# A two-layer hybrid decoder on one core: a new ordering model, turned forms by TensorE and ScalarE, and GpSimd's products on VectorE

## The chip, the cores and the metric

The kernel runs on one core of a Trainium2 chip. The metric is the device time of one execution in microseconds, from the first instruction to the last with what lies around them; lower is better. A run is one execution, and the number quoted for a kernel is the median of its runs. The engines have short names in the rows: PE is TensorE (PEld its weight loads), DVE is VectorE, ACT is ScalarE, POOL is GpSimd, SP is the queue that issues the DMAs.

## The reference

Two layers work on a residual stream of 512 tokens by 1024 channels. Each layer projects the stream once and gives the result to four token mixers on their own heads: A is a gated delta rule in chunks of 64 tokens, B is attention with low-rank queries and keys, C is a gated linear recurrence (HGRN2), D is dilated attention over three windows. Their outputs are joined, projected back and normalised, and a feed-forward block of width 4096 follows.

```python
for l in range(DEPTH):
    h = x @ w_in[l]
    ...
    o_a = _gated_deltanet(a_qkv, a_a, a_b, a_z, gdn_conv_w[l], gdn_a_log[l], gdn_dt_bias[l], gdn_norm_g[l])
    o_b = _mla(b_cq, b_ckv, b_kr, mla_q_norm_g[l], mla_kv_norm_g[l], mla_w_uq[l], mla_w_ukv[l], pos)
    o_c = _hgrn2(c_q, c_f, c_i, c_g, lower_bounds[l], hgrn_norm_g[l])
    o_d = _dilated_attention(d_qkv)
    mixed = jnp.concatenate([o_a, o_b.astype(x.dtype), o_c, o_d], axis=-1) @ w_out[l]
    x = _layer_norm(DEEPNORM_ALPHA * x + mixed, ln1_g[l], ln1_b[l])
    x = _layer_norm(DEEPNORM_ALPHA * x + _sq_relu_mlp(x, w_ff1[l], w_ff2[l]), ln2_g[l], ln2_b[l])
```

Inside A each chunk inverts a unit lower triangular matrix of 64 by 64, and the state runs from chunk to chunk.

## The kernel before

Activations lie with channels on the 128 partitions and the 512 tokens along the row. Every large product is made of three (high by high, high by low, low by high) from a split of both factors into a rounded part `H` and a rest `L`; `wh` and `wl` are the two parts of a weight tile, `xH` and `xL` those of the stream, and `mm`, `a`, `b`, `o` are the names of the eight PSUM buffers by use. A weight tile costs a DMA (`wr`), a rounding on ScalarE (`wh`) and a subtraction on VectorE (`wl`).

The program is first recorded as a list of operations with their dependences. A planner then goes through a model of the engines in time and picks, step by step, the operation that can start first. Its ties and its preferences come from a priority: the place in the list plus a `BIAS` by mixer and engine. `FILL`, `EMA`, `BURST`, `PATIENCE` and `DENSE` tell it when to prefer products of the full array, and `HOP`, `LEAVE`, `ENTER`, `WINDOW`, `DOWN`, `UP` are the figures of its model. The order found is then emitted engine by engine and fixed; on the chip each engine runs its own list from the front, and semaphores do the rest. So a number in the planner moves instructions all over the program, and no instruction overtakes another of its engine at run time.

The steps that the prediction speaks of, by their tile names:

- `sqh`, `sql`: the two parts of the squares for the norms of B; TensorE sums them over partitions (`a<-sqh,oner`, `a<-sql,oner`).
- `ktok`, `vtok` (mixer A) and `vt`, `kt` (mixer C): token-major forms, for each chunk of 64 tokens a 64 by 64 matrix turned on both halves of the partitions. `to_tokens` makes each with eight VectorE transposes of 32-row blocks. `ke` and `kd` are `ktok` times decays.
- `dt`, `db`, `LT`, `N`, `X`, `W`, `TB`, `T`, `U`: the decay matrices of A and the inverse of its triangular matrix. VectorE inverts blocks of 16 in 15 steps, writes `T` and `U` by block transposes, and TensorE then joins the blocks by small products (`a<-T,N`, `a<-Y,U`, `a<-U,Y`, `a<-T,LT`). The prediction calls this the `T` step.
- `qh`: the queries of B, products of PSUM tiles with a table on VectorE.
- `qa`, `kr`, `tot`, `sc`: queries, keys, running decay and scores of C, in six levels (`b<-qa,kr` are its score products).
- `at`, `as`, `tt`: scores, sums and turned weights of both attentions; `dk`, `dq`, `dl`, `dv` and `dtab` belong to D.
- `gm`: the gated output of A and C, split into `mixH` and `mixL` for the output projection.
- `o<-wh,mixH` and the like: the last of the three groups of the output projection, which the layer norm (`xt`, `lns`, `lny`) of the same 128 tokens follows.

GpSimd does elementwise products: `gm`, `qd`, `dt`, `db`, `t`, `N`, `kd`, `st`, `fl`, `kr`, `tot`.

```python
key = (t, e == "pe" and (dense or 0 < run < BURST) and ops[i][9] < DENSE, ops[i][8])
if pick is None or key < pick[0]:
    pick = (key, i, new)
```

Of the kernel before, what the change touches and what calls it, by code (L numbers as in the profile page):

```python
# [10 lines left out]
FR = mybir.dt.float32r  # L11
# [148 lines left out]
class Plan:  # L160
# [4 lines left out]
    TO_PE = 70.0  # L165
    LEAVE, ENTER = 95.0, {(128, 128): 105.0}
    WINDOW, DOWN, UP = 3413.0, 0.29, 0.65

    def __init__(self, nc):
        self.nc, self.ops, self.tiles = nc, [], 0  # L170
        self.kinds, self.queues, self.stream, self.bias = {}, {}, "", 0
        self.quota, self.reserve, self.fifo = {}, {}, set()
        self.ties, self.tied = {}, None
# [33 lines left out]
    def cost(self, e, method, out, ins, k):  # L207
        n = math.prod(out.shape[1:])
        psum = any(v.buf.kind == "ps" for v in [out, *ins])
        if e == "pe":  # L210
            if method == "transpose":
                return 109.0
            w, x = k["lhsT"], k["rhs"]
            n, m = math.prod(x.shape[1:]), w.shape[1]
            if w.dt == FR:
                return max(n * 0.4167 + 13.5, 109.0)
            t = 2 * max(2 * n * 0.4167 + 3, 2 * min(m, n) * 0.4167 + 3, 25.0)
            if w.shape[0] <= 64 or m <= 64:
                return t - 12 if out.span()[0] < 64 else 12.0
            return t  # L220
        if e == "ve":
            if method == "transpose":
                wide = len(out.shape) > 2 and out.shape[1] == 8
                return 446.0 if wide else 1045.0
            if method in ("tensor_scalar", "tensor_copy") and not psum:
                return 64 + 0.52 * n
            if method == "memset":
                return 30.0
            if method == "reciprocal":
                return 68 + 6.3 * n  # L230
            if method == "scalar_tensor_tensor" and not psum and n > 64:
                return 95 + 1.1 * n
            if method == "tensor_tensor_reduce":
                return 195 + 1.045 * n
            return 67 + 1.045 * n
        if e == "ac":
            if method == "dma_start":
                return 60.0
            ap = sum(not isinstance(k.get(w, 0.0), (int, float)) for w in ("bias", "scale"))
            acc = 90.0 if k.get("accum_out") is not None else 0.0  # L240
            return (51 if psum else 93) + (60 * ap if n <= 128 and psum else 93 * ap) + acc + 0.833 * n
        if e == "po":
            if method == "tensor_scalar":
                return 150 + 4.2 * n
            return 190 + 2.2 * n
        return 450.0

    def tile_of(self, method, k):
        if method == "transpose":
            return (128, 128)  # L250
        if method != "matmul":
            return None
        grid = lambda c: 32 if c <= 32 else 64 if c <= 64 else 128
        return grid(k["lhsT"].shape[0]), grid(k["lhsT"].shape[1])

# [7 lines left out]
    def record(self, e, method, a, k):  # L263
# [8 lines left out]
        ins = [v for v in [*a[1:], *k.values()] if isinstance(v, View) and not any(v is o for o in outs)]  # L272
# [32 lines left out]
        if self.tied is not None and e.name == "pe":  # L305
            self.tied.append(i)
        self.ops.append([e, method, a, k, deps, list(bufs.values()), cost, tail, i + self.bias + BIAS.get((self.stream, e.name), 0),
                         self.activity(e, method, k, cost), self.tile_of(method, k)])

    def order(self):  # L310
# [18 lines left out]
        warm, dense, mode, run, forced = False, True, None, 0, None  # L329
# [44 lines left out]
        while done < n:  # L374
            best = None
            for e, cand in avail.items():
                pick = None
                for i in cand if forced is None or e != "pe" else (forced,):
                    t = max(at[e], ready[i])
                    new = [b for b in ops[i][5] if not b.held]  # L380
# [20 lines left out]
            t = max(at[e], ready[i])  # L401
            for kd in {b.kind for b in new}:
                t = max(t, sorted(slots[kd])[sum(b.kind == kd for b in new) - 1])
# [9 lines left out]
            if e == "pe":  # L413
# [5 lines left out]
                if not warm:  # L419
                    cost, work = 2 * cost, 2 * work  # L420
                if mode is not None and op[10] != mode:
                    t = max(t, at[e] + self.LEAVE)
                    cost += self.ENTER.get(op[10], 50.0)
                mode, forced = op[10], self.ties.get(i)
                run = run + 1 if op[9] >= DENSE else 0
                busy += work
                gap = math.exp(-(t - at[e]) / EMA)
# [3 lines left out]
            at[e] = t + cost  # L431
            self.warm[i] = warm
            end[i] = at[e]
# [9 lines left out]
            for j in users[i]:  # L443
# [6 lines left out]
                ready[j] = max(ready[j], end[i] + lat)  # L450
# [24 lines left out]
def emit(ctx, tc, io, layers=DEPTH):  # L475
# [133 lines left out]
    for l in range(layers):  # L609
# [6 lines left out]
        def gated(ot, gate, gain, k, tag):  # L616
# [7 lines left out]
            po.tensor_tensor(m, ot, sq, OP.mult)  # L624
# [108 lines left out]
        kq = [big("kq", [128, 8, 2, 64]) for _ in range(2)]  # L733
        vtok, z = [None, None], [None, None]
        bx = row("bx")
        def a_proj(name, o=None):
# [31 lines left out]
            dst = kq[p][:, :, 1 if name[1] == "q" else 0, :]  # L768
# [83 lines left out]
        for p in range(2):  # L852
# [10 lines left out]
            po.tensor_tensor(v3(qd[p]), kq[p][:, :, 1, :], v3(eg), OP.mult)  # L863
# [4 lines left out]
            po.tensor_tensor(v3(dt), v3(dt), rep(incl), OP.mult)  # L868
            db = row("db")
            po.tensor_tensor(v3(db), v3(dt), spread(beta[:, :, p]), OP.mult)  # L870
            QK[p] = row("QK")
            for nh in range(2):
                o = ps("a", (128, 4, 2, 64))
                for i in range(4):
                    for h in range(2):
                        b = kq[p][half[h], 4 * nh + i]
                        pe.matmul(o[half[h], i], lhsT=b[:, 0, :], rhs=b, start=True, stop=True)
# [49 lines left out]
        po.tensor_tensor(t1[r], bx[r], qtab[r], OP.mult)  # L927
        po.tensor_tensor(t2[r], bx[r], ktab[r], OP.mult)
# [47 lines left out]
        for p in range(2):  # L976
# [3 lines left out]
            po.tensor_tensor(Nv, pn(LT, p), rep(lev), OP.mult)  # L980
# [21 lines left out]
            to_tokens(v3(ktok), kq[p][:, :, 0, :])  # L1002
            ve.tensor_tensor(v3(ke), v3(ktok), spread(ce[:, 0, :, p]), OP.mult)
            po.tensor_tensor(v3(kd[p]), v3(ktok), spread(ce[:, 1, :, p]), OP.mult)
# [8 lines left out]
        for n in range(8):  # L1013
# [28 lines left out]
            else:  # L1042
                po.tensor_tensor(new, st, spread(ce[:, 2, n]), OP.mult)
# [22 lines left out]
        for name in W_TILES[9:17]:  # L1066
# [4 lines left out]
            if name[1] == "f":  # L1071
# [4 lines left out]
                po.tensor_tensor(fl, fl, e, OP.add)  # L1076
# [8 lines left out]
            elif name[1] == "i":  # L1085
# [3 lines left out]
                to_tokens(v3(vt[p]), v3(t))  # L1089
# [7 lines left out]
        for p in range(2):  # L1097
# [10 lines left out]
            for i in range(6):  # L1108
# [18 lines left out]
                po.tensor_tensor(kv[:, :, 0], kv[:, :, 0], spread(tv[:, :, 1], b), OP.mult)  # L1127
                nt_ = plan.tile("row" if nb > 64 else "sm", [128, nb], FT, "tot")
                po.tensor_tensor(nt_, tv[:, :, 0], tv[:, :, 1], OP.mult)
                tot = nt_  # L1130
            kt = row("kt")
            to_tokens(v3(kt), v3(kr[p]))
# [296 lines left out]
```

## Time and profile before

| | |
|---|---|
| median of three runs | 1382.39 us (1381.54 to 1384.11) |
| the profiled execution | 1383.82 us, span of its instructions 1382.0 us |
| mean granted clock of TensorE | 0.985 |
| busy: TensorE, VectorE, ScalarE, GpSimd | 1336.3, 784.7, 596.6, 91.4 us |

The span runs from the first to the last instruction of the profiled execution; the difference to its own time is what lies around it. An engine is busy while an instruction of its own runs; waiting for a semaphore is idle time, and the trace names the engine whose work ended it. Products on TensorE overlap, so the length of one says less than the distance from one start to the next. Layer 0 runs to about 675 us, and its feed-forward block begins at about 350 us.

### The profile page before, as it was taken

Reading aid. Unit: us, or ns where it says so; the run is one execution under the profiler, and the core shown is the slowest. Engines: PE = TensorE matmul, PEld = TensorE weight load, DVE = VectorE, ACT = ScalarE, POOL = GpSimd, SP = SyncE. Lnnn points to the kernel's source line nnn. Section 1 sums busy time; section 2 is a strip of 40 time slices with the busy share of each in tenths; the row PEclk is TensorE's granted clock in tenths of the full one; section 3 lists DMA queues with packets and bytes.
Section 4 is the critical chain, followed back from the end, with each engine's and each line's share of the span. In section 5 each row is a group of like instructions: output and inputs, shape, how many; then the busy total and the mean of one; then the engine's idle time right before and its main releaser. Section 6 shows DMA issues by size and latency. Waiting matters only on the chain.

```text
span 1382.0 us, 21797 instructions
## 1 busy us (share of the span) xinstructions
PE 1336.3 (97%) x8860; PEld 1084.0 (78%) x8860; DVE 784.7 (57%) x1533; ACT 596.6 (43%) x1124; POOL 91.4 (7%) x108
## 2 busy tenths in 40 slices
PE   8899999999999999999998989999999999999997
PEld 7657778778888888888886678787788888888886
DVE  6989585567743334422479898846658333344226
ACT  6643456548432223321485434656374322233112
POOL 0222020010000000000003212200000000000000
PEclk9999999999999999999999999999999999999999
DMA  6122201232542223324122242021415323232341
GB/s 225 40 88 77 82 4 47 77 122 74 165 141 93 92 92 94 105 92 155 59 92 62 92 146 71 3 69 69 135 64 189 116 92 92 92 106 92 126 149 61
DMA packets 44164, 132.65 MB, mean 96 GB/s; under 512 B 4896, under 2 KB 5152, under 8 KB 44064
## 3 DMA queue, kind: packets, MB, share of 16 engines
q1 hardware_dynamic: 44064, 131.27, 29.5%
q8 instruction: 69, 1.13, 0.3%
q14 instruction: 31, 0.25, 0.1%
HBM read 122.86 MB, written 8.39 MB: 95 GB/s over the span
## 4 chain that ended last, share of the span: by engine, by line
PE 76%; DVE 14%; ACT 7%; issue 2%; DMA 1%; POOL 0%; SPq 0%; DVEq 0%; POOLq 0%; ACTq 0%
PE mm L472 42%; PE a L472 17%; PE b L472 16%; ACT lny L472 2%; DVE wl L472 1%; DVE xt L472 1%; DVE y L472 1%; ACT wh L472 1%; DVE vtok L472 1%; PE o L472 1%; DVE ktok L472 1%; ACT scr L472 1%; ACT sg L472 1%; ACT xH L472 1%; DVE X L472 1%
## 5 line engine op out<-in xcount | busy, mean ns | idle before, releaser
L472 DVE TENSOR_TENSOR wl<-wr,wh 128x1024 fp32r<-128x1024 f32 (+1 forms) x195 | 237.6, 1222 | 360.4 <-ACT wh L472 355.1
L472 ACT ACTIVATE wh<-wr 128x1024 fp32r<-128x1024 f32 (+1 forms) x195 | 204.7, 1054 | 528.6 <-PE mm L472 501.1
L472 PE MATMUL mm<-xH,wl 128*128 128x512 f32 (+1 forms) x832 | 328.0, 395 | 0.0
L472 PE MATMUL mm<-xL,wh 128*128 128x512 f32 (+1 forms) x832 | 326.6, 393 | 0.0
L472 PE MATMUL mm<-xH,wh 128*128 128x512 f32 (+1 forms) x832 | 325.7, 392 | 0.7 <-DVE as L472 0.4
L472 PEld LDWEIGHTS mm<-xH,wh 128*128 128x128 f32 x832 | 157.9, 190 | 38.1 <-issue 1.9
L472 PEld LDWEIGHTS mm<-xL,wh 128*128 128x128 f32 x832 | 157.5, 190 | 38.1 <-issue 2.3
L472 PEld LDWEIGHTS mm<-xH,wl 128*128 128x128 f32 x832 | 157.6, 190 | 34.8 <-issue 1.6
L472 DVE TENSOR_TENSOR hL<-h,hH 128x512 fp32r<-128x512 f32 x64 | 41.8, 687 | 73.4 <-PE mm L472 73.2
L472 PE MATMUL b<-wh,hL 128*128 128x512 f32 x192 | 74.8, 390 | 0.0
L472 PE MATMUL b<-wh,hH 128*128 128x512 f32 x192 | 74.8, 390 | 0.0
L472 PE MATMUL a<-wh,hH 128*128 128x512 f32 x192 | 74.8, 389 | 0.0
L472 PE MATMUL a<-wl,hH 128*128 128x512 f32 x192 | 74.8, 389 | 0.0
L472 PE MATMUL b<-wl,hH 128*128 128x512 f32 x192 | 74.7, 389 | 0.0
L472 PE MATMUL a<-wh,hL 128*128 128x512 f32 x192 | 74.7, 389 | 0.0
L472 PE MATMUL mm<-wh,hH 128*128 128x512 f32 x128 | 49.9, 390 | 0.0
L472 PE MATMUL mm<-wh,hL 128*128 128x512 f32 x128 | 49.8, 389 | 0.0
L472 PE MATMUL mm<-wl,hH 128*128 128x512 f32 x128 | 49.8, 389 | 0.0
L472 ACT ACTIVATE at<-at,as 128x512 f32<-128x512 f32 (+3 forms) x64 | 35.7, 558 | 27.6 <-DVE as L472 27.5
L472 ACT ACTIVATE hH<-h 128x512 fp32r<-128x512 f32 x64 | 37.3, 619 | 15.4 <-DVE h L472 15.2
L472 DVE TENSOR_TENSOR h<-h,mm 128x512 f32<-128x512 f32 x60 | 40.6, 680 | 3.6 <-ACT h L472 3.6
L472 PEld LDWEIGHTS a<-wl,hH 128*128 128x128 f32 x192 | 36.1, 188 | 7.6
(292 smaller groups left out, 2275.8 us busy)
## 6 DMA issues: line engine op xcount, KB each, us to landing
wr<-in_w_ff_dram SPq DMA_DIRECT2D x128, 512.0 KB, 3.6
wr<-in_w_in_dram SPq DMA_DIRECT2D x47, 512.0 KB, 3.6
wr<-in_w_out_dram SPq DMA_DIRECT2D x16, 512.0 KB, 3.6
x<-xt SPq DMA_DIRECT2D x24, 256.0 KB, 2.1
xt<-x SPq DMA_DIRECT2D x24, 256.0 KB, 5.8
ln<-in_ln_dram SPq DMA_DIRECT2D x16, 256.0 KB, 5.5
x<-in_xT_dram SPq DMA_DIRECT2D x8, 256.0 KB, 6.1
dtab<-in_tabs_dram SPq DMA_DIRECT2D x8, 256.0 KB, 4.0
```

Source lines behind the costliest of these rows:

```text
L472: getattr(e.real, method)(*[real(v) for v in a], **{n: real(v) for n, v in k.items()})
```

## The change

There are three parts. First, the planner's model and its numbers: a matrix product now holds only the 32 by 32 cells of the array that it uses, so that products on other cells may follow at once; VectorE and GpSimd wait for each other in the model where an operation `shares` their port; activity of TensorE is counted by `streaming`; and `FILL`, `BURST`, `DOWN`, `UP` and `BIAS` have new values. Second, `turn` takes the place of `to_tokens` in four places: four TensorE transposes of 128 by 128 into one PSUM tile, and four ScalarE copies of 64 rows by 256 columns out of it; `kq` is laid out with keys and queries apart. Third, all products of GpSimd are VectorE's; GpSimd keeps only the fills of `TB`, `T` and `U`.

```diff
-FILL = (0.3, 0.5)
+FILL = (0.2, 0.30000000000000004)
 EMA = 2000.0
-BURST = 2
+BURST = 1
...
-BIAS = {('A0', 'ac'): -50, ('B', 've'): 600, ('C0', 've'): 200, ('D', 'ac'): -200}
+BIAS = {('', 've'): -750, ('A', 'po'): -800, ('A', 've'): 50, ('A0', 'ac'): 500, ('A0', 've'): 300,
...
-    WINDOW, DOWN, UP = 3413.0, 0.29, 0.65
+    WINDOW, DOWN, UP = 3413.0, 0.36, 0.38
...
+    def shares(self, e, method, ins, out):
+
+        inside = [v for v in ins if v.buf.kind != "ps"]
+        if e == "po":
+            return bool(inside)
+        if e != "ve":
+            return False
+        return len(inside) > 1 or (method in ("tensor_scalar", "tensor_copy") and len(inside) == 1 and out.buf.kind != "ps")
...
+    def streaming(self, e, method, k):
+
+        if e.name != "pe":
+            return 0.0
+        if method == "transpose":
+            return 107.0
+        w, n = k["lhsT"], math.prod(k["rhs"].shape[1:])
+        return n * 0.4167 * (1 if w.dt == FR else 4) * w.shape[0] / 128
...
+                    if e == "pe":
+                        t = max(t, drained) if turn else max(t, max(free[c] for c in ops[i][12]))
...
+    def turn(dst, src, tag):
+
+        o = ps(tag, (128, NT, 128))
+        for m in range(NT):
+            pe.transpose(o[:, m], src[:, 128 * m:128 * m + 128], ident)
+        d = dst.rearrange("q (m c) i -> q m c i", c=2)
+        for h in range(2):
+            for c in range(2):
+                ac.activation(d[half[h], :, c], o[half[c], :, 64 * h:64 * h + 64], AF.Copy)
...
-            po.tensor_tensor(m, ot, sq, OP.mult)
+            ve.tensor_tensor(m, ot, sq, OP.mult)
...
-        kq = [big("kq", [128, 8, 2, 64]) for _ in range(2)]
+        kq = [big("kq", [128, 2, 8, 64]) for _ in range(2)]
...
-                to_tokens(v3(vtok[p]), v3(y))
+                turn(v3(vtok[p]), y, "a")
...
-            po.tensor_tensor(v3(qd[p]), kq[p][:, :, 1, :], v3(eg), OP.mult)
+            ve.tensor_tensor(v3(qd[p]), kq[p][:, 1], v3(eg), OP.mult)
...
-            po.tensor_tensor(v3(dt), v3(dt), rep(incl), OP.mult)
+            ve.tensor_tensor(v3(dt), v3(dt), rep(incl), OP.mult)
...
-            po.tensor_tensor(Nv, pn(LT, p), rep(lev), OP.mult)
+            ve.tensor_tensor(Nv, pn(LT, p), rep(lev), OP.mult)
...
-            to_tokens(v3(ktok), kq[p][:, :, 0, :])
+            turn(v3(ktok), kq[p][:, 0].rearrange("q n i -> q (n i)"), "a")
...
-                po.tensor_tensor(kv[:, :, 0], kv[:, :, 0], spread(tv[:, :, 1], b), OP.mult)
+                ve.tensor_tensor(kv[:, :, 0], kv[:, :, 0], spread(tv[:, :, 1], b), OP.mult)
...
-            to_tokens(v3(kt), v3(kr[p]))
+            turn(v3(kt), kr[p], "b")
```

Three places of the order show what moves. In each row stand the operation, what it writes from what, and the shape of what it writes (a count at the end for equal rows in a run).

The first place is VectorE in mixer A and B's norms of layer 0, some 75 rows into its list. Before:

```order
L472 TENSOR_TENSOR dt<-a,ct_635 128x512
L472 TENSOR_SCALAR dt<-dt 128x512
L472 TENSOR_TENSOR ke<-ktok,ce 128x512
L472 STREAM_TRANSPOSE ktok<-kq 32x8x32 x4
L472 TENSOR_TENSOR sql<-bsq,sqh 128x512
L472 TENSOR_TENSOR ke<-ktok,ce 128x512
L472 TENSOR_TENSOR wl<-wr,wh 128x1024
L472 TENSOR_TENSOR sql<-bsq,sqh 128x512
```

And now, at the second `sql` of that shape:

```order
L522 TENSOR_TENSOR wl<-wr,wh 128x1024
L522 TENSOR_TENSOR sql<-bsq,sqh 128x512
L522 SCALAR_TENSOR_TENSOR kq<-y,sq 128x512
L522 TENSOR_TENSOR dt<-a,ct_628 128x512
L522 TENSOR_TENSOR qd<-kq,eg 128x512
L522 TENSOR_TENSOR dt<-a,ct_628 128x512
L522 TENSOR_TENSOR qd<-kq,eg 128x512
L522 TENSOR_SCALAR dt<-dt 128x512 x2
L522 SCALAR_TENSOR_TENSOR cn<-mm,par,bsq 128x512
L522 TENSOR_TENSOR dt<-dt,cc 128x512 x2
```

The `ktok` transposes have left VectorE, both `sql` come ahead of the `dt` products, both `ke` stand some 40 rows later, and `qd` and `dt<-dt,cc`, which were GpSimd's, are rows of VectorE.

The second place is TensorE at the `T` step of layer 0, 442 rows into its list before and 417 now. Before:

```order
L472 MATMUL mm<-xH,wh 128x512
L472 MATMUL a<-T,N 64x64 x32
L472 MATMUL a<-Y,U 64x64 x16
L472 MATMUL a<-U,Y 64x64 x16
L472 MATMUL a<-Y,U 64x64 x16
L472 MATMUL a<-U,Y 64x64 x16
L472 MATMUL mm<-xL,wh 128x512
L472 MATMUL mm<-xH,wl 128x512
L472 MATMUL a<-T,LT 32x32 x32
```

And now:

```order
L522 MATMUL mm<-xH,wl 128x512
L522 MATMUL a<-T,N 64x64 x32
L522 MATMUL b<-qa,kr 64x64
L522 MATMUL a<-Y,U 64x64 x16
L522 MATMUL a<-U,Y 64x64 x16
L522 MATMUL a<-Y,U 64x64 x16
L522 MATMUL a<-U,Y 64x64 x16
L522 MATMUL b<-qa,kr 64x64 x31
L522 MATMUL a<-T,LT 32x32 x32
```

Scores of C stand where two products of a projection (`mm`) stood. Ahead of `a<-T,N` the lists hold 280 products `mm` of projections before and 249 now in layer 0, and 278 and 269 in layer 1.

The third place is TensorE in the dilated attention D of layer 0. Before, between its turned weights (`b<-cc,at`) and its products with the values (`b<-tt,dv`):

```order
L472 MATMUL b<-tt,dv 64x128 x4
L472 MATMUL a<-sqh,bdr 128x512
L472 MATMUL mm<-xH,wh 128x512
L472 MATMUL b<-cc,at 128x128 x3
L472 MATMUL mm<-xL,wh 128x512
L472 MATMUL mm<-xH,wl 128x512
L472 MATMUL b<-cc,at 128x128
```

And now:

```order
L522 MATMUL b<-cc,at 128x128 x4
L522 MATMUL o<-wh,mixL_2876 128x512
L522 MATMUL o<-wh,mixH_2833 128x512
L522 MATMUL o<-wl,mixH_2833 128x512
L522 MATMUL b<-cc,at 128x128 x4
L522 MATMUL o<-wh,mixL_2840 128x512
L522 MATMUL o<-wh,mixH_2869 128x512
L522 MATMUL o<-wl,mixH_2869 128x512
```

D stood among the projections of `az`, ahead of the whole output projection; now the first two groups of the output projection come before it, and it shares its stretch with the last group `o` and, after that, the first feed-forward products.

## Rows read from the trace of the kernel before

**Rows 1.** The page, its part 1: busy time, share, instructions.

```profile
PE 1336.3 (97%) x8860; PEld 1084.0 (78%) x8860; DVE 784.7 (57%) x1533; ACT 596.6 (43%) x1124; POOL 91.4 (7%) x108
```

**Rows 2.** Waits of TensorE: who for whom, us in total, times, longest.

```profile
PE a L472 <- DVE sql L472: 7.7, 4, 3.1
PE a L472 <- DVE T L472: 7.0, 4, 2.0
PE a L472 <- ACT wh L472: 5.9, 1, 5.9
PE mm L472 <- DVE xt L472: 3.4, 3, 1.6
PE a L472 <- DVE as L472: 3.0, 4, 1.0
PE b L472 <- DVE qh L472: 2.9, 1, 2.9
PE a L472 <- DVE xt L472: 1.8, 5, 0.4
PE b L472 <- DVE kt L472: 1.5, 1, 1.5
```

**Rows 3.** Three stretches: length, busy PE, PEld, DVE, ACT, POOL, clock, DMA.

```profile
25.00:150.00 125.00, 115.38 (x882) 86.53 (x882) 109.93 (x205) 64.76 (x108) 26.86 (x28) 0.95 0.25 76
350.00:675.00 325.00, 325.00 (x1452) 267.03 (x1451) 124.57 (x147) 97.22 (x126) 0.00 (x0) 1.00 0.36 114
675.00:835.00 160.00, 151.07 (x926) 117.28 (x926) 134.99 (x268) 90.62 (x166) 26.58 (x26) 0.96 0.27 89
```

**Rows 4.** The same view of seven stretches at the low clock, with their sum.

```profile
63.60:70.40 6.80, 5.68 (x12) 3.64 (x12) 6.77 (x10) 0.00 (x0) 2.20 (x2) 0.50 0.22 77
128.40:135.30 6.90, 5.75 (x108) 5.75 (x109) 4.89 (x11) 2.25 (x3) 0.00 (x0) 0.51 0.01 3
258.10:261.60 3.50, 3.50 (x12) 2.74 (x11) 3.46 (x18) 2.12 (x7) 0.00 (x0) 0.51 0.02 9
753.10:759.90 6.80, 5.56 (x14) 4.00 (x13) 6.33 (x11) 3.04 (x5) 2.49 (x2) 0.50 0.49 154
...
sum 37.90, PE 32.60 PEld 27.22 DVE 33.78 ACT 13.56 POOL 4.69; mean PE 4.66 PEld 3.89 DVE 4.83 ACT 1.94 POOL 0.67
```

**Rows 5.** Timeline, 60 to 66 us: start, length, instruction, idle time before.

```profile
59.98 1.45 POOL L472 TENSOR_TENSOR dt<-dt,cc 128x512 f32<-128x512 f32 x1 [1.02 <-ACT dt L472]
60.21 1.77 DVE L472 TENSOR_TENSOR ke<-ktok,ce 128x512 f32<-128x512 f32 x1
...
62.00 1.80 DVE L472 STREAM_TRANSPOSE ktok<-kq 32x256 f32<-32x256 f32 x4
...
64.72 0.79 PE L472 MATMUL a<-sql,oner 128*128 128x512 f32 x1 [3.12 <-DVE sql L472]
...
65.31 0.63 PE L472 MATMUL mm<-xL,wh 128*128 128x512 f32 x1
...
65.73 0.63 PE L472 MATMUL mm<-xH,wl 128*128 128x512 f32 x1
```

**Rows 6.** Groups of VectorE: count, busy us, mean ns, idle before.

```profile
L472 DVE STREAM_TRANSPOSE ktok<-kq 32x256 f32<-32x256 f32 x32 | 13.9, 436 | 0.6
...
L472 DVE TENSOR_TENSOR QK<-a,dt 128x256 f32<-128x256 f32 x8 | 3.0, 411 | 0.0
...
L472 DVE TENSOR_TENSOR dt<-a,ct 128x512 f32<-128x512 f32 x4 | 2.7, 683 | 0.1
```

**Rows 7.** A copy group of ScalarE; timeline of TensorE, eight transposes.

```profile
L472 ACT ACTIVATE tt<-b 128x256 f32<-128x256 f32 x16 | 5.8, 390 | 2.0 <-PE b L472 1.9
...
334.73 1.11 PE L472 MATMUL a<-cc,xt 128*128 128x128 f32 x8 [0.33 <-DVE xt L472]
```

**Rows 8.** Timeline of TensorE where the tile shape changes.

```profile
141.62 0.40 PE L472 MATMUL mm<-xH,wl 128*128 128x512 f32 x1
141.95 1.20 PE L472 MATMUL a<-U,Y 32*32 32x32 f32 x64
```

More of the change, by code (lines that the diff above doesn't have):

```diff
@@ L254, in tile_of, with cells @@
         return grid(k["lhsT"].shape[0]), grid(k["lhsT"].shape[1])
+    def cells(self, method, a, k):
+        if method == "transpose":
+            return tuple(range(16))
+        rows, cols = self.tile_of(method, k)
+        r, c = k["lhsT"].span()[0] // 32, a[0].span()[0] // 32
+        return tuple(4 * i + j for i in range(r, r + rows // 32) for j in range(c, c + cols // 32))
+    def streaming(self, e, method, k):
+        if e.name != "pe":
+            return 0.0
+        if method == "transpose":
+            return 107.0
+        w, n = k["lhsT"], math.prod(k["rhs"].shape[1:])
+        return n * 0.4167 * (1 if w.dt == FR else 4) * w.shape[0] / 128
     def activity(self, e, method, k, cost):
@@ L271, in record @@
             outs.append(k["accum_out"])
-        ins = [v for v in [*a[1:], *k.values()] if isinstance(v, View) and not any(v is o for o in outs)]
+        ins = [v for v in [*a[1:7], *(v for w, v in k.items() if w not in ("out", "accum_out"))] if isinstance(v, View)]
         if method == "copy_predicated" or (method == "matmul" and not k["start"]):
@@ L328, in order @@
         dma_at = win = busy = ema = 0.0
-        warm, dense, mode, run, forced = False, True, None, 0, None
+        warm, dense, mode, run, forced, ports = False, True, None, 0, None, {"ve": 0.0, "po": 0.0}
+        free, drained = [0.0] * 16, 0.0
         self.warm = [True] * n
@@ L420, in order @@
                     cost, work = 2 * cost, 2 * work
+                busy += op[13]
                 if mode is not None and op[10] != mode:
-                    t = max(t, at[e] + self.LEAVE)
+                    t = max(t, drained + self.LEAVE)
                     cost += self.ENTER.get(op[10], 50.0)
+                else:
+                    t = max(t, max(free[c] for c in op[12]))
+                self.start[i] = t
                 mode, forced = op[10], self.ties.get(i)
                 run = run + 1 if op[9] >= DENSE else 0
-                busy += work
-                gap = math.exp(-(t - at[e]) / EMA)
+                gap = math.exp(-max(0.0, t - drained) / EMA)
                 keep = math.exp(-cost / EMA)
@@ L430, in order @@
                 dense = not warm or ema < (FILL[1] if dense else FILL[0])
-            at[e] = t + cost
+            at[e] = end[i] = t + cost
+            if op[11]:
+                ports[e] = at[e] - self.PORT
             self.warm[i] = warm
-            end[i] = at[e]
+            if e == "pe":
+                drained = max(drained, end[i])
+                for c in op[12]:
+                    free[c] = end[i]
+                if len(op[12]) < 16:
+                    at[e] = t + self.ISSUE
             if op[7]:
@@ L875, in emit @@
                     for h in range(2):
[L876 to L877 removed]
+                        b = kq[p][half[h], :, 4 * nh + i]
+                        pe.matmul(o[half[h], i], lhsT=b[:, 0], rhs=b, start=True, stop=True)
                 ns = slice(4 * nh, 4 * nh + 4)
@@ L1042, in emit @@
             else:
-                po.tensor_tensor(new, st, spread(ce[:, 2, n]), OP.mult)
+                ve.tensor_tensor(new, st, spread(ce[:, 2, n]), OP.mult)
                 ve.tensor_tensor(new, new, o, OP.add)
@@ L1088, in emit @@
                 vt[p] = row("vt")
-                to_tokens(v3(vt[p]), v3(t))
+                turn(v3(vt[p]), t, "b")
             else:
```

31 lines of the change are left out of this document (19 added, 12 removed), and 4 rows, old and new, of the table BIAS.

## The prediction

> **What bounds the kernel now.** I read the page first, then the waits of TensorE, then busy time by stage, then the stretches at the low clock. The page gives PE 1336.3 us of a span of 1382.0 [rows 1]: TensorE is the bound, and only its losses can be won. The feed-forward stage of layer 0 has none: 1452 products in 325.00 us, 0.224 us each, at clock 1.00 [rows 3]. The two front halves of the mixers do lose: 25 to 150 us is busy for 115.38 of 125, 675 to 835 us for 151.07 of 160, at mean clocks of 0.95 and 0.96, and there VectorE is busy for 109.93 and 134.99 us [rows 3]. VectorE is therefore the engine that TensorE waits for in these stretches.
>
> The waits say the same. The seven rows ended by VectorE hold 7.7 + 7.0 + 3.4 + 3.0 + 2.9 + 1.8 + 1.5 = 27.3 us; the one large wait on ScalarE, 5.9 us, is the start of the program, which the change leaves as it is [rows 2]. I split the 27.3: front (`sql`, `T`, `qh`, `kt`) 19.1 us, back (`xt`, `as`: dilated attention, output projection, layer norm) 8.2 us.
>
> The second loss is the clock. Seven stretches, 37.90 us together, ran at 0.50 to 0.52 of full speed, with TensorE busy for 32.60 us of them [rows 4]. A 512-column product starts 0.42 us after the one before it there (65.31, then 65.73 [rows 5]) against 0.224 above, so the level is 1.2 instead of 2.4 GHz and costs up to half of the busy time, 16.3 us. The first stretch begins inside a wait: TensorE stood 3.12 us for `sql`, while VectorE did a `ke` of 1.77 us and four block transposes ahead of it [rows 5]. The second, 128.4 to 135.3, follows the wait for `T`.
>
> **VectorE's load.** 128 block transposes go: four groups of 32 at 0.436 us (one group is shown [rows 6]), 55.8 us. `ke`, of the same size as the others, takes 1.77 us while GpSimd runs `dt` beside it [rows 5]; a product of that size without GpSimd takes 0.683 [rows 6], so the four `ke` alone lose 4.3 us to the neighbour. What comes over from GpSimd is 96 products: 36 of 512 columns (the 32-row `t` among them) at 0.683, 24.6 us; 24 `kr` of 256 at 0.411, 9.9 us; 12 `st` of 128 columns and 24 `tot` of 8 to 256, which I bound from above by the 256-column row, 14.8 us, and take at half, 7 us. In sum 784.7 - 55.8 - 4.3 + 41.5 = 766 us. What matters more is where: in the front, `ktok` and `vtok` alone were 14 us of each layer's chain before `T`, and up to twelve products of 0.683 (8.2 us) take their place.
>
> By the Trainium skill, page "SBUF — State Buffer", section "Who interferes with whom", a VectorE instruction with two SBUF inputs and a GpSimd one that reads SBUF hold one port in turn, each for its whole length. This trace agrees as far as `ke` goes (1.77 us beside GpSimd); by that rule every product moved also takes a blocker away, and the saving would be larger than my 4.3 us.
>
> **ScalarE.** 64 copies of 64 rows by 256 columns are new. The nearest row is `tt` of 256 columns, 0.390 us [rows 7]: 25 us more on an engine that is busy 596.6 of 1382 [rows 1]. I cost them at nothing, as ScalarE is idle for 60 of the 125 us of the front [rows 3]; without that cover each form would stand for 4 x 0.390 = 1.6 us, against eight block transposes of 3.5 us before, so even uncovered it is not later.
>
> **TensorE.** 64 transposes of 128 by 128 are new, all on the path. Eight in a row take 1.11 us from the first start to the last end [rows 7]: 8.9 us more for the 64. That is the upper bound, and I take it; the lower is nothing, if all fell into waits.
>
> **The new order.** Counted over all rows of the order, TensorE changes its tile shape 165 times instead of 182. The product before a change of shape at 141.62 us is followed after 0.33 us [rows 8] instead of 0.224: 0.1 us each, 1.7 us won. In the first place shown of the order, the row that writes `sql` stood behind `ke` and four transposes, and now stands before the `dt` products; ahead of TensorE's `sql` there is then nothing long on VectorE. In the second place TensorE reaches the `T` step with 31 big products (7 us) fewer before it in layer 0, 9 fewer in layer 1, while VectorE has lost 14 us of transposes and taken up 8.2 us, and each of its products is rid of GpSimd as neighbour; the wait for `T` should shrink, not vanish. `qh` waited behind six `vtok` transposes that are gone, and `kt` no longer is eight steps of VectorE. Of the 19.1 us in front I take 17.1 as won, all but one wait at `T` as long as the longest now, 2.0 us [rows 2] (bounds: none, and all). The 8.2 us at the back I leave.
>
> The clock follows the waits. I let the first low stretch of each layer go with its wait for `sql` (5.68 and, in layer 1, 5.56 busy, half of each: 5.6 us; [rows 4] show the first). The `T` step stays mostly of small tiles, 64 rows by 64, as the second place shows, and keeps its low stretch. Of the three short ones, 3.50 us busy each, I let half go: 2.6 us. That makes 8.2 us (bounds 0 and 16.3).
>
> The third place is a cost. Dilated attention, which had projections between its steps, now stands among the `o` products of the last output group, right ahead of the layer norms that need it. I add nothing for it in the sum, because those products are independent of the attention's next step; a rival prices it.
>
> **Sum.** -17.1 - 8.2 - 1.7 + 8.9 = -18.1 us. The profiled execution took 1383.82 us (span 1382.0, 1.8 us around it), 1.4 us above the median of 1382.39 of the runs shown. So 1365.7 for such an execution, and **1364.3 us** as median, 1.3% faster. From no change a measurement of this kernel can tell about 0.2%, 2.8 us; the three runs shown lie within that.
>
> **Rivals.**
> *All waits go* (1343 to 1356). If TensorE's waits on VectorE vanish in front and back, with all the low stretches: -27.3 - 16.3 - 1.7 + 8.9 = -36.4, 1346 us. For it: 27.3 of the waits hang on one engine that is unloaded. Against it: the back is not unloaded, and the `T` step keeps its small tiles. Chance 0.20.
>
> *The last group waits* (1373 to 1381). Each of the eight row blocks (four in a layer) needs, one after the other, attention, output product, layer norm. If each waits 1.5 us longer, half of the 3.12 us that `sql` cost, that is 12 us, and the sum is -6.1: 1376.3. For it: the third place. Against it: 24 `o` products and later feed-forward ones per block as cover. Chance 0.14.
>
> *The waits only move* (1381 to 1385). TensorE waits for ScalarE's copies where it waited for VectorE's transposes, and the won order pays for the 8.9 us: 1382. It takes a ScalarE that is late by what VectorE was; its 60 idle us speak against it. Chance 0.08.
>
> *Slower: the clock* (over 1385). The `T` step now runs its small tiles without the two big products that split them, 31 `qk` scores of 64 rows follow at once, and the turned forms bring transposes where projections stood. Each further stretch as the first, 6.80 us with 5.68 busy, costs 2.8 us. To eat up 18.1 us takes more than six of them, with the present ones still there more than three (18.1 - 8.2 = 9.9). With five and the old ones kept: 1382.4 - 9.9 + 14 = 1386.5. For it: the stretch at 128.4 already belongs to the `T` step. Against it: the 31 products saved there are spread through the later small-tile stretch. Chance 0.14. The Trainium skill's page "TensorE: Matmul & The Clock Gate", section "Part 4: PE-mode transpose", speaks for this rival: a transpose does not count as work for the clock. No run here shows that by itself: the stretch at 258.1 follows waits and score products as well.
>
> My own case (1356 to 1373) has the rest, 0.44. **Chances**: faster by over 0.2% is 0.44 + 0.20 + 0.14 = 0.78, within 0.2% 0.08, slower 0.14. **Range**: 1346 to 1386 leaves out the far end of the first rival (about 0.04) and most of the last (about 0.12); my own case by itself is 1356 to 1373.
>
> **What would show it.** The waits of TensorE: no `sql` of 3 us, `T` under 3 us in all, `qh` gone; ScalarE as releaser under 10 us. The clock row: no low stretch near 60 and 750 us, one at each `T` step. VectorE busy near 766 us or below, more below if GpSimd slowed more than `ke`. If `xt`, `as` or `mixL` hold 15 us or more, the last group was the price; if the low stretches sum to over 45 us, the clock was. Wrong altogether would be a front whose idle time stays at 9 us a layer although VectorE has fallen by the transposes: then the order, not VectorE's load, set these waits.

## The result and the profile after

The changed kernel takes **1347.01 us** (median of four runs, 1346.60 to 1347.33) against 1382.62 (1381.54 to 1384.11) beside it: ratio 0.9742 [0.9725, 0.9758], 2.6% faster. The forecast was 1364.3, and 1356 to 1373 for the own case; the time lies below that, 1 us above the 1346 of the rival "All waits go". The profiled execution has a span of 1345.5 us against 1382.0.

Page of the changed kernel, its part 1 (before: [rows 1]):

```profile
PE 1322.3 (98%) x8924; PEld 1075.2 (80%) x8924; DVE 738.4 (55%) x1501; ACT 614.0 (46%) x1188; POOL 4.7 (0%) x12
```

TensorE was idle for 1382.0 - 1336.3 = 45.7 us and is idle for 1345.5 - 1322.3 = 23.2: of the 36.5 us won, 22.5 are idle time and 14.0 busy time. VectorE is 46 us lighter.

Waits of TensorE, changed kernel, who for whom (before: [rows 2]):

```profile
PE a L522 <- ACT wh L522: 5.7, 1, 5.7
PE a L522 <- DVE T L522: 2.3, 2, 1.3
PE mm L522 <- ACT xH L522: 1.8, 2, 0.9
PE a L522 <- DVE xt L522: 1.4, 4, 0.4
PE o L522 <- ACT lny L522: 1.1, 2, 0.6
PE b L522 <- DVE as L522: 0.8, 1, 0.8
...
PE b L522 <- DVE T L522: 0.4, 1, 0.4
PE a L522 <- DVE sql L522: 0.2, 1, 0.2
```

The seven rows ended by VectorE in [rows 2] held 27.3 us; all such rows hold 5.1 now. In front 19.1 became 2.3 + 0.4 + 0.2 = 2.9: `qh` and `kt` are gone, `sql` is at 0.2, `T` is left. At the back 8.2 became 1.4 + 0.8 = 2.2. ScalarE's copies brought no wait of their own: the largest row is still the start.

The same stretches as in [rows 3], where the stages now lie, and the `T` step of layer 0; length, busy PE, PEld, DVE, ACT, POOL, clock, DMA:

```profile
25.00:150.00 125.00, 123.75 (x1159) 95.08 (x1158) 97.48 (x201) 75.45 (x141) 1.84 (x2) 1.00 0.25 77
...
660.00:815.00 155.00, 152.70 (x1276) 121.72 (x1276) 126.82 (x263) 101.76 (x200) 0.00 (x0) 1.00 0.31 99
...
104.00:126.00 22.00, 20.75 (x429) 17.95 (x428) 16.66 (x25) 6.46 (x14) 1.84 (x2) 1.00 0.17 54
```

The front of layer 0 loses 1.25 us of 125 (9.62 before), that of layer 1 2.3 of 155 (8.93 of 160 before). None of the seven low stretches of [rows 4] is left; the clock is at 2.4 GHz to the last product. The `T` step too runs at 1.00, though its tiles are what they were. Timeline of TensorE there:

```profile
111.08 0.32 PE L522 MATMUL a<-T,N 64*64 64x64 f32 x2
112.66 2.08 PE L522 MATMUL a<-T,N 64*64 64x64 f32 x62 [1.25 <-DVE T L522]
```

One wait of 1.25 us, then 7.6 us of products of 64 rows (to 120.3), with no fall. What the parts cost: groups of VectorE and ScalarE (before: [rows 5 to 7]),

```profile
L522 DVE TENSOR_TENSOR ke<-ktok,ce 128x512 f32<-128x512 f32 x4 | 2.7, 686 | 0.0
...
L522 ACT ACTIVATE vtok<-a 64x256 f32<-64x256 f32 x16 | 6.0, 378 | 0.2
```

and TensorE's timeline at one of the turns, eight transposes in a row:

```profile
86.32 1.04 PE L522 MATMUL a<-cc,y 128*128 128x128 f32 x8
```

### The profile page after: what moved, and what is told of

Read it like the earlier page. It is cut to its first block, busy times and chain, and to the rows that moved or that the text cites. A ratio compares the mean times of both kernels' runs of the same rounds, so it can differ in the third digit from the quotient of the medians.

```text
span 1345.5 us, 21777 instructions
## 1 busy us (share of the span) xinstructions
PE 1322.3 (98%) x8924; PEld 1075.2 (80%) x8924; DVE 738.4 (55%) x1501; ACT 614.0 (46%) x1188; POOL 4.7 (0%) x12
## 4 chain that ended last, share of the span: by engine, by line
PE 83%; DVE 10%; ACT 5%; issue 1%; DMA 0%; DVEq 0%; SPq 0%; ACTq 0%
PE mm L522 47%; PE a L522 18%; PE b L522 15%; PE o L522 3%; ACT lny L522 2%; DVE xt L522 1%; DVE wl L522 1%; ACT wh L522 1%; DVE U L522 1%; DVE T L522 1%; ACT xH L522 1%; DVE y L522 0%; DVE kh L522 0%; ACT sg L522 0%; ACT scr L522 0%
## 5 line engine op out<-in xcount | busy, mean ns | idle before, releaser
L522 PE MATMUL mm<-xL,wh 128*128 128x512 f32 (+1 forms) x832 | 321.8, 389 | 0.0
L522 PE MATMUL mm<-xH,wl 128*128 128x512 f32 (+1 forms) x832 | 320.1, 387 | 0.0
L522 PEld LDWEIGHTS b<-wh,hL 128*128 128x128 f32 x192 | 36.0, 188 | 7.5
```

Source lines behind the costliest of these rows:

```text
L522: getattr(e.real, method)(*[real(v) for v in a], **{n: real(v) for n, v in k.items()})
```

## The experiments

All times are medians with the ratio to the kernel before on the same chip. Three questions: which part of the change gives the 35 us, what the clock hangs on, and what the transposes cost.

### The three parts, one by one and in pairs

The first four runs keep the old model and its numbers, or the new model and the old operations.

**Turned forms alone** (`e1_turn_old_order`). The kernel before with:

```diff
-                to_tokens(v3(vtok[p]), v3(y))
+                turn(v3(vtok[p]), y, "a")
...
-            to_tokens(v3(kt), v3(kr[p]))
+            turn(v3(kt), kr[p], "b")
```

and `ktok`, `vt`, `kq` likewise. "Old order" here and below means the old planner with its numbers: it plans each kernel's list anew, so a run compares two lists and not only two sets of operations.

> The turned forms alone, with the ordering model, its numbers and GpSimd's products of before. Load theory (what VectorE has to do sets TensorE's waits, whatever the order): 128 block transposes, 56 us of VectorE, are gone, so about half of the 35.6 us of the whole change: 1365 us. Order theory (the model and its numbers set them): 1378 to 1390 us, because TensorE has 64 transposes more and the order is as blind as before. Neighbour theory (GpSimd beside VectorE is what made VectorE late): 1375 us, with ke still at 1.7 us.

Measured 1374.99 (1373.43 to 1376.12), 0.9952 [0.9937, 0.9967]. That is the time of "neighbour", but without its sign: `ke` is at 0.68 us although GpSimd keeps its products. TensorE waits 0.6 us for `sql` and still 5.8 for `T`, and four low stretches are left (about 24 us). None of the three theories is borne out.

**Products alone** (`e2_products_old_order`). The kernel before, with each `po.tensor_tensor` written `ve.tensor_tensor`.

> GpSimd's 96 products on VectorE alone, with to_tokens and the ordering model of before. Neighbour theory: VectorE's instructions are all at their own length (ke 0.69 us), its busy time stays near 785 us or falls, and the time falls by half of the change or more: 1365 us or less. Load theory: VectorE gets 40 us of products and loses about 30 of slow ones, so no gain: 1378 to 1388 us. Order theory: 1378 to 1388 us.

Measured 1397.06 (1392.64 to 1397.91), 1.0102 [1.0083, 1.0121]. Waits of TensorE:

```profile
PE a L472 <- DVE sql L472: 17.5, 4, 13.0
...
PE b L472 <- DVE kt L472: 2.9, 1, 2.9
```

Timeline of VectorE and TensorE around the longest of them:

```profile
86.29 0.69 DVE L472 TENSOR_TENSOR ke<-ktok,ce 128x512 f32<-128x512 f32 x1
86.89 3.58 DVE L472 STREAM_TRANSPOSE vtok<-y 32x256 f32<-32x256 f32 x8
90.62 0.69 DVE L472 TENSOR_TENSOR kd<-ktok,ce 128x512 f32<-128x512 f32 x1
91.35 0.69 DVE L472 TENSOR_TENSOR sql<-bsq,sqh 128x512 fp32r<-128x512 f32 x1
...
92.09 0.80 PE L472 MATMUL a<-sql,oner 128*128 128x512 f32 x1 [12.98 <-DVE sql L472]
```

Window of the first of its five low stretches:

```profile
82.60:106.50 23.90, 14.41 (x19) 5.63 (x20) 20.70 (x50) 7.61 (x12) 0.00 (x0) 0.50 0.17 45
```

`ke` is down to 0.69 us, so the neighbour is gone; but VectorE's own list is longer, and `sql` stands behind `kd`, which was GpSimd's, and the block transposes. TensorE stood 13 us for it, and 23.9 us at half clock lie around the wait. No theory had the kernel slower by 15 us; VectorE's busy time rose by only 12.3 (to 797.0).

**Both operations, old order** (`e3_both_old_order`): both edits above.

> Turned forms and products on VectorE together, with the ordering model and numbers of before: all of the change but its order. Load and neighbour theories: 1350 to 1360 us, nearly the whole gain, VectorE busy for 738 us as in the changed kernel. Order theory: 1372 to 1385 us, with waits on VectorE of 15 us or more and low stretches still there.

Measured 1358.91 (1357.71 to 1359.39), 0.9835 [0.982, 0.985]. "Load and neighbour" holds: 22.6 us (against 1381.53 beside it) of the 35.6 come without the new order. Wait of TensorE for `T`, and the two fronts over the same stretches as in [rows 3]:

```profile
PE a L472 <- DVE T L472: 1.7, 2, 0.9
...
25.00:150.00 125.00, 123.25 (x1081) 91.90 (x1081) 93.36 (x195) 76.21 (x139) 1.85 (x2) 1.00 0.24 77
675.00:835.00 160.00, 157.96 (x1395) 123.19 (x1393) 124.86 (x259) 99.60 (x190) 0.00 (x0) 1.00 0.29 96
```

The fronts lose 1.75 and 2.04 us, `sql` is at 0.2, and the `T` step runs at clock 1.00. So under the old planner the two operations alone free the front. What they leave is at the back: the waits for `as` and `xt` hold 7.0 us, and the two low stretches left (244.5 to 251.3 and 920.3 to 923.7) lie in D.

**The order alone** (`e4_order_alone`): the changed kernel with `to_tokens`, the old `kq` and GpSimd's products.

> The new model and its numbers over the operations of before (block transposes, products on GpSimd). Order theory: 1350 to 1365 us. Load and neighbour theories: 1375 to 1390 us, as VectorE's work of 785 us and its slow instructions are those of before, and the numbers were chosen for another program.

Measured 1364.30 (1360.30 to 1365.15), 0.9870 [0.9853, 0.9886]. "Order" holds. `sql` is down to 0.3 us and `T` to 4.0 with VectorE nearly as loaded as before (775.3 us busy against 784.7), but TensorE now waits for other late tiles of VectorE and ScalarE (`vn` 2.4, `U` 2.3, `sc` 1.6), and three low stretches are left in layer 1 (about 24 us). The waits for `as` and `xt` are down to 2.7 us.

The next two take one operation out of the changed kernel.

**Products back on GpSimd** (`e5_new_order_gpsimd`): `ve.tensor_tensor` written `po.tensor_tensor` again for the moved products.

> The changed kernel, only that the 108 products of GpSimd go back to it; the new model keeps its rule that VectorE and GpSimd wait for each other. Theory 'the neighbour': GpSimd's reads slow VectorE, and no order avoids it. Then VectorE loses the 41 us of the products but gets back some 29 us of slowing (what was missing between 784.7 + 41.5 and the 797.0 us of the kernel of before with the products moved alone), so it is near 725 us, `ke` is over 1.0 us again, and TensorE waits for VectorE over 15 us instead of 5: about 1363 us, which is 16 above the changed kernel, as the products were worth 16.1 us under the old order with the turned forms in place (1374.99 to 1358.91). Rival 'the model': the new planner places GpSimd's products where VectorE reads PSUM or rests. Then VectorE is near 700 us, `ke` near 0.7 us, waits on VectorE stay under 8 us, and the time is 1347 to 1351 us.

Measured 1345.55 (1345.42 to 1346.20), 0.9736 [0.9721, 0.975]. Page, part 1:

```profile
PE 1321.9 (98%) x8924; PEld 1075.5 (80%) x8924; DVE 719.4 (54%) x1405; ACT 614.8 (46%) x1188; POOL 91.3 (7%) x108
```

Waits of TensorE:

```profile
PE a L522 <- ACT wh L522: 5.3, 1, 5.3
...
PE b L522 <- ACT kt L522: 1.4, 2, 0.7
PE a L522 <- ACT tt L522: 1.2, 1, 1.2
PE a L522 <- DVE xt L522: 1.2, 3, 0.4
```

"The neighbour" falls, "the model" holds: with the turned forms and the new order the move of the products is worth nothing. VectorE is only 19.0 us lighter without them, near the 725 us of "the neighbour", though the rows of the 96 products (count times mean length of their groups) sum to 44.1 us in the changed kernel. Summed in the same way, the other rows are 9.9 us longer here, beside GpSimd (four `qa` of 256 columns, for one, take 785 ns and not 417); the other 15 us are rows that overlap, which busy time counts once. No wait hangs on that, and the `T` waits are gone. `ke` is at 0.68 us: no GpSimd product runs beside any of the four.

**Block transposes back** (`e6_new_order_block_transposes`): `turn` out again in all four places, products on VectorE.

> The changed kernel, only that the four token-major forms are made by VectorE's block transposes again (128 of them, 0.436 us each, 56 us more on VectorE; 64 TensorE transposes less, 8.3 us at 1.04 us for eight). Theory 'the load': in the front VectorE, which was busy for 97 of 125 us in layer 0 and 127 of 155 in layer 1, gets 28 us more in each and becomes the bound there: waits on VectorE of 20 us and more, low clock after them, 1375 us or more. Under the old order the same step was worth 38 us (1397.06 to 1358.91). Rival 'the order': the planner, which knows the transposes, spreads them over stretches where VectorE rests, waits on VectorE stay under 10 us, and the 8.3 us won on TensorE stay: 1340 to 1350 us.

Measured 1381.92 (1380.92 to 1385.90), 1.0001 [0.9991, 1.0011]. Waits of TensorE:

```profile
PE mm L522 <- DVE wl L522: 8.0, 3, 5.3
PE a L522 <- DVE T L522: 7.3, 1, 7.3
...
PE b L522 <- DVE kt L522: 5.0, 3, 2.4
```

Window of the longest of its five low stretches:

```profile
799.00:819.50 20.50, 12.88 (x109) 11.23 (x110) 20.41 (x34) 3.72 (x7) 0.00 (x0) 0.50 0.70 231
```

"The load" holds: with the products on VectorE and without the turned forms the whole gain is gone (with the products on GpSimd 18 us of it stay, `e4_order_alone`). Even `wl`, which every projection needs, comes late. VectorE is busy for 20.41 of the 20.50 us at 799.

The eight corners, medians in us:

| | old operations | turned forms | products moved | both |
|---|---|---|---|---|
| old order | 1382.6 | 1375.0 | 1397.1 | 1358.9 |
| new order | 1364.3 | 1345.6 | 1381.9 | 1347.0 |

The order is worth 12 to 29 us in every column. The turned forms are worth 8 to 19 us while GpSimd keeps its products, and 35 to 38 where VectorE has them. The move of the products wins 16 us in one corner only (old order, turned forms), costs 14 to 18 without the turned forms, and in the new order with them costs 1.5 us, at the edge of what can be told. So order and turned forms give the whole gain (1345.6), and both operations without the order give two thirds of it (1358.9). Each corner is one list of its planner; how much of a difference hangs on that one list no run shows.

### The clock

**A late `T`** (`e7_late_T`). The changed kernel in its own order; each `Z` is written five times.

```diff
-            getattr(e.real, method)(*[real(v) for v in a], **{n: real(v) for n, v in k.items()})
+            times = 5 if method == "tensor_scalar" and a[0].buf.name == "Z" else 1
+            for _ in range(times):
+                getattr(e.real, method)(*[real(v) for v in a], **{n: real(v) for n, v in k.items()})
```

> The changed kernel with the same order, only that VectorE writes each of the four `Z` of a layer five times (sixteen useless instructions of 0.31 us a layer, 5.0 us), so that `T` comes 5 us later. Theory 'the clock follows waits': TensorE waits for `T` some 12 us instead of 2.3 in all, and after each of the two waits the clock stays at the lower level for one stretch of about 6.8 us, 2.8 us each: 1347 + 10 + 6 = 1363 us. Rival 'the clock is set by what TensorE runs there': the small tiles of the `T` step are the same as in the changed kernel, in which they ran at clock 1.00, so no low stretch comes: 1357 us. Third: later work has slack and the planner's order hides half of the delay: 1352 us.

Measured 1363.71 (1362.59 to 1364.49), 0.9868 [0.9852, 0.9885]: 16.7 us slower than the changed kernel. Waits of TensorE:

```profile
PE a L524 <- DVE T L524: 15.2, 4, 6.1
```

TensorE's timeline at the `T` step of layer 0:

```profile
116.44 0.45 PE L524 MATMUL a<-T,N 64*64 64x64 f32 x2 [6.15 <-DVE T L524]
118.46 3.57 PE L524 MATMUL a<-T,N 64*64 64x64 f32 x61 [1.57 <-DVE T L524]
```

Windows of the low stretches, one in each layer:

```profile
115.20:122.10 6.90, 4.09 (x70) 3.93 (x71) 6.07 (x11) 0.60 (x1) 0.00 (x0) 0.51 0.18 47
794.50:804.70 10.20, 4.85 (x66) 4.48 (x67) 10.07 (x14) 3.29 (x5) 0.00 (x0) 0.50 0.61 180
```

"The clock follows waits" holds: the same products in the same order ran at 1.00 behind a wait of 1.25 us and at 0.51 behind waits of 6.15 and 1.57; 62 of them took 2.08 us and 61 now take 3.57. That the time meets the 1363 foretold is in part luck, as two sizes were off against each other: idle time rose by 12.0 us, not 10, and TensorE's busy time by 3.3, not 6. How much waiting it takes is not settled by this run: the kernel before has a low stretch at its `T` step with waits of 1.39 and 1.79 us.

### The transposes

**Every transpose twice** (`e8_turn_twice`). The changed kernel in its own order; as above, with `times = 2` for the transposes of `turn`.

> The changed kernel with the same order, only that each of the 64 TensorE transposes of the turned forms is issued twice into the same place of PSUM (the copies stay as they are). Theory 'a price on the path': eight in a row took 1.04 us in the changed kernel, so 64 more take 8.3 us and nothing else moves: 1355.3 us, clock 1.00 throughout. Rival 'the clock': transposes let the clock fall; then at one or more of the eight turns a low stretch of some 7 us appears, 2.8 us each: 1358 us with one, 1378 us with all eight. Rival 'they lie in waits': 1347 to 1350 us.

Measured 1349.90 (1349.64 to 1352.67), 0.9771 [0.9756, 0.9786]: 2.9 us more. Groups of TensorE in the changed kernel:

```profile
L522 PE MATMUL b<-cc,kr 128*128 128x128 f32 x16 | 2.6, 276 | 0.1
L522 PE MATMUL b<-cc,ci 128*128 128x128 f32 x16 | 2.4, 274 | 0.4 <-DVE T L522 0.4
L522 PE MATMUL a<-cc,kq 128*128 128x128 f32 x16 | 2.2, 272 | 0.0
L522 PE MATMUL a<-cc,y 128*128 128x128 f32 x16 | 2.1, 272 | 0.0
```

and with every transpose twice:

```profile
L525 PE MATMUL b<-cc,kr 128*128 128x128 f32 x32 | 4.4, 274 | 0.3 <-DVE kr L525 0.3
L525 PE MATMUL b<-cc,ci 128*128 128x128 f32 x32 | 4.1, 274 | 0.0
L525 PE MATMUL a<-cc,kq 128*128 128x128 f32 x32 | 4.0, 273 | 0.0
L525 PE MATMUL a<-cc,y 128*128 128x128 f32 x32 | 3.8, 273 | 0.0
```

The turn of `y` shown above, eight transposes in 1.04 us, is now

```profile
86.06 1.91 PE L525 MATMUL a<-cc,y 128*128 128x128 f32 x16
```

The groups grow from 9.3 to 16.3 us, 0.109 us for each of 64 transposes; TensorE's busy time as a whole rose by 4.9 (to 1327.2), and where the other 2.1 went no run shows. TensorE comes to the `T` step later, its waits for `T`, 2.7 us, are gone, and only 2.9 us show in the time, which is that of "they lie in waits". No low stretch came, though up to 16 transposes stood in a row, so "the clock" falls.

### Model or numbers, and a better version

**The changed kernel again** (`e9_changed_again`), as it is, beside the next three.

> The changed kernel as it is, on the chip on which the next three are timed, so that differences of 1 to 2 us can be told. Theory 'the products are worth nothing under the new order': it is within 1.5 us of 1345.55, the time with the products on GpSimd. Rival 'they cost a little': it is 1346.5 to 1347.5 again, over 1 us above it, in line with 2.3 us more of waits for `T`, which that kernel has not. Third: under 1344.5, then VectorE is the better place after all.

Measured 1346.60 (1345.87 to 1347.77), 0.9739 [0.9724, 0.9753]; 1.05 us above the kernel with GpSimd's products, whose interval overlaps. The first two theories both allow this and are not told apart; the third is out.

**New model, old numbers** (`e10_model_with_old_numbers`).

```diff
-FILL = (0.2, 0.30000000000000004)
+FILL = (0.3, 0.5)
...
-BURST = 1
+BURST = 2
...
+BIAS = {('A0', 'ac'): -50, ('B', 've'): 600, ('C0', 've'): 200, ('D', 'ac'): -200}
```

> The changed kernel, only that `FILL`, `BURST` and `BIAS` have their values of before (the new model, turned forms and products on VectorE stay). It tells whether the new order's gain comes from the model or from the numbers that go with it. Under the old model, with the same operations and these numbers, the time was 1358.91 us, and with the new model and the new numbers 1347.0. Theory 'the numbers': 1356 to 1362 us, with TensorE's waits near 20 us and one or two low stretches. Theory 'the model': 1345 to 1350 us, waits near 15 us, none.

Measured 1351.37 (1350.31 to 1352.51), 0.9775 [0.9759, 0.9792]. Waits of TensorE:

```profile
PE a L518 <- DVE as L518: 3.1, 4, 1.0
PE a L518 <- DVE T L518: 2.9, 2, 1.6
PE a L518 <- DVE xt L518: 2.0, 6, 0.4
PE mm L518 <- DVE xt L518: 1.1, 2, 0.6
PE mm L518 <- DVE as L518: 0.7, 1, 0.7
```

Windows of its two low stretches:

```profile
243.50:246.90 3.40, 3.40 (x9) 2.52 (x9) 2.76 (x13) 2.74 (x8) 0.00 (x0) 0.50 0.28 113
912.50:915.90 3.40, 3.40 (x10) 2.65 (x9) 3.40 (x17) 2.04 (x7) 0.00 (x0) 0.50 0.01 2
```

Between both theories: the model gives 7.5 us of the 12.3 between 1358.91 and 1346.6, the numbers 4.8. Here D's products with the values (`b<-tt,dv`) lie at 251.7 to 266.1 us, ahead of the whole output projection (269.7 on), as in the kernel before; in the changed kernel they lie at 280 to 313, within the last group `o` (271 to 318). The front waits are as in the changed kernel (`T` 2.9), while the back keeps 3.1 + 2.0 + 1.1 + 0.7 = 6.9 us in the rows shown and a low stretch ahead of these products in each layer. No run moves D alone, but the other kernels agree: with the old numbers (the kernel before, `e1` to `e3`, this one) D comes ahead of the output projection and the waits for `as` and `xt` hold 6.3 to 9.0 us; with the new ones it lies in the last group, in both layers, and they hold 1.2 to 3.1, whatever the operations. So the place of D, which the numbers set, most likely freed the back.

**Block transposes for one form** (`e11_gpsimd_kt_blocks`, `e12_gpsimd_vt_blocks`). The kernel of `e5_new_order_gpsimd` with one line more:

```diff
-            turn(v3(kt), kr[p], "b")
+            to_tokens(v3(kt), v3(kr[p]))
```

or the same for `vt`.

> The changed kernel with the products back on GpSimd, and with `kt` alone made by VectorE's block transposes again (32 of them, 14 us of VectorE, 16 TensorE transposes less). A try for a version below both kernels: with GpSimd's products VectorE was busy for 719 us and TensorE waited for `kt` 1.4 us by ScalarE's copies. If VectorE has room in this stretch, TensorE saves 16 transposes of 0.109 us, 1.7 us, and part of the wait: 1342 to 1344.5 us. Theory 'the load' (the block transposes were worth 35 us in all four forms with the products on VectorE): `kt` comes late, and it is 1348 us or more.

> The same with `vt` alone made by VectorE's block transposes again (32 of them, 14 us of VectorE, 16 TensorE transposes less), products on GpSimd. `vt` is wanted late, long after its source is there. If VectorE has room: 1.7 us less, 1343 to 1344.5 us. If 14 us more on VectorE delay `T` or `kr` behind them: 1348 us or more.

Measured 1346.88 (1346.36 to 1346.91), 0.9739 [0.9725, 0.9754] for `kt`, with a wait for `kt` of 0.9 us on VectorE and a low stretch at 183.9 to 187.3: nothing won, and neither theory's time. For `vt` 1344.85 (1344.37 to 1346.20), 0.9727 [0.9713, 0.9742]: the lowest median of all, 1.75 us below the changed kernel on the same chip, though one run of each lies within the other's. Page, part 1, of the second:

```profile
PE 1319.9 (98%) x8908; PEld 1074.1 (80%) x8908; DVE 733.7 (55%) x1437; ACT 609.5 (45%) x1172; POOL 90.0 (7%) x108
```

Against the first line of `e5_new_order_gpsimd` TensorE is 2.0 us less busy, VectorE 14.3 more, and nothing waits for `vt`: this form, which is wanted late, cost nothing on VectorE. The time is just above the 1343 to 1344.5 foretold, and the gain over the changed kernel is no more than can be told.

## Why the prediction was right in kind and too small

The direction and the bound were right; the waits at the back and the clock were mis-sized, and the transposes a little. All in us of the profiled span:

| step of the prediction | predicted | found |
|---|---|---|
| front waits (`sql`, `T`, `qh`, `kt`) | -17.1 | -16.2 |
| back waits (`xt`, `as`) | 0 | -6.0 |
| clock | -8.2 | -16.3 (upper bound, not measured apart) |
| tile shape changes | -1.7 | -1.6 (189 to 173 in the trace, at the same 0.1) |
| 64 transposes | +8.9 | +7.0 |
| sum | -18.1 | -33.1 of -36.5 |

The rival "All waits go" had -36.4, by luck in part: 5.1 us of its waits stayed, its transposes were 1.9 too dear, and 3.4 us are in none of its terms.

- **"Of the 19.1 us in front I take 17.1 as won"**: right in size, and so were `sql` and `qh` gone and `T` under 3 us. The reason, VectorE's load, is enough: the two operations under the old planner bring `sql` to 0.2, `T` to 1.7 and the fronts to 1.75 and 2.04 us of idle time (`e3_both_old_order`). But it is not the only way: the order alone takes `sql` from 7.7 to 0.3. One part by itself leaves `T` at 4.0 (order) or 5.8 (turned forms). The prediction's test for "the order, not the load" did not allow for both.
- **"The 8.2 us at the back I leave"** and **"I add nothing for it in the sum"**, of D among the last `o` products: the first failed step. The back fell to 2.2 us. With D among the products of the last group the attention's steps are covered; with D ahead of the output projection again (`e10_model_with_old_numbers`) the waits are back at 7.4 us. The rival "The last group waits" had the place right and the sign wrong.
- **"The `T` step ... keeps its low stretch"** and **"of the three short ones ... I let half go"**: the second failed step. The prediction tied the low clock there to the small tiles. The late `T` shows that waiting ahead of them brings it: with 1.25 us none, with 6.15 and 1.57 us one. The other traces agree: one wait of 0.8 to 1.6 us at this step, no low stretch (changed kernel, `e3`, `e10`); two waits, 1.4 to 3.0 and 0.9 to 1.8 us, one (the kernel before, `e1`, layer 1 of `e4`). Two of the short ones (258.1 and 944.2) began up to 1.5 us after waits for `as` in D, the third (879.4) during the products behind a wait of 1.49 us for `kt`. Length alone does not tell: in `e10` waits of 1.05 and 0.50 us in D were followed by a low stretch. All seven went, 16.3 us by half of the busy time in [rows 4].
- **VectorE at 766 us**: 738.4. "More below if GpSimd slowed more than `ke`" is what happened. With the products moved alone VectorE rose by 12.3 us where 41.5 were worked out: summed by groups, the products' rows are 44.0 us, the other rows became 21.7 us shorter (4.3 were taken for `ke`), and the rest is overlap. The prediction added and took off lengths of rows, but rows overlap: before, they sum to 852.4 us where 784.7 are busy. The rule of the Trainium skill (page "SBUF — State Buffer", section "Who interferes with whom"), by which the prediction expected more than 4.3 us, agrees with the 21.7. In time the move is worth nothing under the new order (`e5_new_order_gpsimd`), and the prediction's "each of its products is rid of GpSimd" gave `T` a reason that it did not need there.
- **ScalarE at nothing**: right. The copies took 0.378 us (0.390 taken), and TensorE's waits for it sum to 9.7 us, of which 5.7 are the start.
- **The transposes** as an upper bound: 7.0 of 8.9, with 2.9 in time where they fall into waits.
- **"Slower: the clock"** did not come, and neither did "The waits only move". The page "TensorE: Matmul & The Clock Gate" of the Trainium skill, "Part 4: PE-mode transpose", says that transposes do not count as work for the clock; no run here tells whether that is so: even twice as many, up to 16 in a row over 1.91 us, made no low stretch (`e8_turn_twice`).

Open are the 3.4 us of the span that the table does not name, 0.3 of them idle and 3.1 busy time: no run was made for them.

## What to carry to other kernels

Where one engine feeds the bound, an order, a lighter load and a moved load are not added up: here one cost 15 us alone, nothing with the others, and won 16 with one of them, so cost them as corners of a table. A wait on TensorE can be paid twice, once as idle time and once as clock behind it, so whoever predicts that a wait goes should let the low stretch behind it go too. Ask of every small chain (here attention and layer norm) which independent large products stand between its steps: here putting it beside them went with fewer waits, where a cost was feared. And do not add lengths of rows to a busy time: rows of one engine overlap.

## What was not expected of the hardware

- The same 64-row products ran at 2.4 GHz for the whole `T` step with 1.25 us of wait ahead, and 61 of them at 1.2 GHz behind 6.15 and 1.57 us; the low level began at 115.2 us, inside the wait that ended at 116.4.
- A float32 transpose of 128 by 128 costs TensorE 0.109 us more when it follows its like (1.91 us for 16, 1.04 for eight), though each by itself is shown with 0.27 us.
- VectorE's `ke` took 1.76 us beside GpSimd and 0.68 to 0.69 with GpSimd idle; but beside GpSimd it is not always slow. In the kernel before, a GpSimd product had begun 0.23 to 0.51 us ahead of each of the four `ke`. In `e4_order_alone` the one `ke` that began 0.51 us behind a GpSimd product took 1.77 us, and the three that began 0.29 to 0.54 us ahead of one took 0.68 to 0.69. So the order decides it, by which of the two comes first.
